# Three layer-norm boundaries of a decoder trunk: two weight residuals ahead of the last norm chain, a reordered first tile, a norm piece cut in two

## The chip, the core and the metric

The kernel runs on one core of a Trainium2 chip. The metric is device time in microseconds (us) of one execution; lower is better. The engines named below are PE (TensorE, matrix products; PEld is its load of the stationary operand), DVE (VectorE), ACT (ScalarE), POOL (GpSimd) and SP (SyncE, which issues nearly all DMAs). Each works through its own instruction list in order and waits on the others by semaphores.

## The reference: what is computed

A two-layer decoder trunk on 256 tokens of width 2048, in float32. Each layer has a token mixer (layer 0 a forgetting attention, "fox"; layer 1 a sliding-window attention, "swa") and a gated feed-forward stage with a short convolution. Every one of the four sub-layers has this form, and the change lies at the joint of two of them:

```python
h = x * (1.0 + sc1) + sh1
y = fox_attention(h, ...)          # or swa_attention, or conv_ffn
x = layer_norm(DEEPNORM_ALPHA * x + (1.0 + g1) * y, ln_mix_g[i], ln_mix_b[i])
h = x * (1.0 + sc2) + sh2
y = conv_ffn(h, ...)
```

The vectors sc, sh and g come from a conditioning vector by a product with a large matrix (`ada_w`), which the kernel forms in the background.

## The kernel before, in words

**Numbers as two parts.** Every float32 operand of a weight product is split into a rounded part and a residual. For a weight pair (two blocks of 128 rows by 512 columns, tile `w`) ACT makes the rounded part `wh` (L276) and DVE the residual `wl = w - wh` (L287). For the activations, `hHL` holds the rounded half hH and the residual half hL, 16 blocks of 128 columns, each by 256 tokens. A product needs three terms: hH by `wh`, hL by `wh`, hH by `wl`. In the feed-forward stages (`w_stationary`, tile `wd`) the weights stand still and hH and hL pass as one operand of 512 columns: 8 products with `wh` of 512 columns and 8 with `wl` of 256 for each pair. In the swa input projection (`x_stationary` with `x_mm`, tile `xs`) the activations stand still: 8 products with `wh` and 4 with `wl`, all of 512 columns.

**The stream.** `stream` issues a pair's load on SP, its rounding on ACT, and puts a closure `go` with its products into the list `work`. `settle(2)` runs the oldest closure while more than two pairs are ahead. Just before a closure runs, `rest` emits the residuals that the next closures need. Tiles `wh` and `wl` have four buffers each (pool `hl`), the loaded `w` ten (pool `wp`).

**The joint.** Between two sub-layers stands a closure put there by `halt` and kept in `stops`: `between`, which calls `modulate`. There are three: fox to feed-forward 0, feed-forward 0 to swa, swa to feed-forward 1. `rest` returns when it meets a stop, so residuals of the next sub-layer's pairs come behind it; those of its first two pairs are in `behind`, which pins them to program order.

**The last norm chain.** The last 512 columns of the old sub-layer's output (`residual` with `end`, L621 to L632) go through DVE token half by token half: times gate, plus x, statistics, aggregate, then POOL raises to the power -1/2. The last pairs of the product before it are kept so that token half 0 ends early (`x_mm_end`). `normalise(d)` (L638) subtracts the mean and scales 512 columns: token half 0 on ACT (L644), token half 1 on DVE (L646). Half 0 of all four pieces runs at once, since ACT comes to them early.

**The modulation.** `modulate` (L500) keeps PE busy with products of ones (`warm`), transposes x blocks 0 to 3 (L508), and `mod_pair(..., fast=True)` makes hHL of them: ACT the rounded half (L478), DVE the whole (L479) and the residual half (L482). The other twelve blocks come two at a time out of the list `feeds`, one with each pair of the new sub-layer: transposes (L469), ACT and DVE (L484, L485), ACT's rounding (L85) and DVE's residual (L86). In front of blocks 4, 8 and 12 stands `norm(k // 4)`, the next 512 columns. `pin` keeps an instruction in program order against other pinned ones; the rest is placed by a scheduler when the kernel is built.

Of the kernel before, what the change touches and what calls it, by code (L numbers as in the profile page):

```python
# [17 lines left out]
P = 128  # L18
# [23 lines left out]
def hybrid_trunk(ctx: ExitStack, tc: tile.TileContext, a: dict, out: bass.AP):  # L42
# [181 lines left out]
    def rest(*items):  # L224

        n = 0
        for f in items:
            if f in stops:
                return
            if f in residuals:  # L230
                residuals[f]()
                n += 1
                if f in behind:
                    return
            elif f in weights:
                n += 1
            if n > 2 - (items[0] not in weights):
                return
# [28 lines left out]

    def stream(wsrc, row0, col, ks, use, spare=0):

        for kc in ks[::2]:  # L270
# [15 lines left out]
            def residual_(w=w, h=h, l=l, go=go):  # L286
                pin(nc.vector.tensor_tensor(l, w, f32(h), op=ALU.subtract), go in behind)  # L287
                del residuals[go]

            if any(f in stops for f in work) and sum(f in behind for f in work) < 2:  # L290
                behind.add(go)
# [5 lines left out]

    def x_mm(ps, kc, h, l, stat, last, first=0, ts=range(NT)):

        for t in ts:  # L300
            for i in range(2):
                xh, xl = stat(kc + i, t)
                mm(ps[t], xh, h[:, i, :], start=kc + i == first)
                mm(ps[t], xl, h[:, i, :])
        feed()
        for t in ts:
            for i in range(2):
                mm(ps[t], stat(kc + i, t)[0], l[:, i, :], stop=kc + i == last)
# [33 lines left out]
    def w_stationary(wsrc, col):  # L342
# [3 lines left out]
        def use(kc, h, l):  # L346
            cells = [(i, f) for i in range(2) for f in range(4)]
            for i, f in cells:
                mm(ps[f], h[:, i, f * P:(f + 1) * P], hHL[:, kc + i].rearrange("p a s -> p (a s)"),
                   start=kc + i == 0)  # L350
            feed()
            for i, f in cells:
                mm(ps[f][:, :S], l[:, i, f * P:(f + 1) * P], hH[:, kc + i, :], stop=kc + i == KC - 1)
# [146 lines left out]
    def modulate(G, B, norm):  # L500

        norm(0)
        warm(10)
        ps = {k: [bank() for _ in range(2)] for k in (0, 2)}
        for t in range(NT):
            for k in ps:
                for j in range(2):
                    pin(nc.tensor.transpose(ps[k][j][:, t * P:(t + 1) * P], x[:, t, (k + j) * P:(k + j + 1) * P], ident))  # L508
            warm(6 - 2 * t)
        for k in ps:  # L510
            mod_pair(G, B, k, [b[:, :S] for b in ps[k]], True)

        def feed_(k):
            if k % 4 == 0:
# [123 lines left out]
    def normalise(d):  # L638

        for t in range(NT):  # L640
            mu, rs, nm = moments[t]
            xs = x[:, t, d * 512:(d + 1) * 512]
            if t == 0:
# [535 lines left out]
```

## Time and profile before

| what | value |
|---|---|
| median of 3 runs | 2253.64 us (2253.16 to 2253.78) |
| the profiled execution | 2253.57 us |
| its span, first to last instruction | 2251.8 us |
| mean granted TensorE clock | 0.996 |
| first joint, fox to feed-forward 0: chain from / first `wd` product | 462.55 / 471.35 us |
| second joint, feed-forward 0 to swa: chain from / first `xs` product | 1216.10 / 1224.18 us |
| third joint, swa to feed-forward 1: chain from / first `wd` product | 1495.64 / 1504.50 us |

The profile is of one execution, and the time around its span is 1.77 us. In a timeline row stand the start and the length in us, the engine, the line, the operation with output and inputs, how many are merged into the row, and in brackets how long the engine had been idle and who released it. A merged row runs from the first start to the last end, and neighbouring instructions of an engine overlap a little. In a row of a stretch stand its bounds and length, the busy time and count of each engine, the granted clock, the DMA share and the rate. In the chain of waits each piece starts where the one before it ends, so its lengths add up.

### The profile page before, as it was taken

The numbers are of one execution on the slowest core, as the hardware profiler recorded it, in microseconds if no ns is written. First come the engines' busy times: TensorE is split into PE (matmuls) and PEld (weight loads), VectorE is DVE, ScalarE is ACT, GpSimd is POOL, SyncE is SP. The second block draws the span as 40 slices with busy tenths as digits, with TensorE's granted clock in tenths as the row PEclk, the third lists the DMA queues.
The fourth block names the chain that finished last, engine by engine and source line by source line (L and its number), as shares of the span: only waits on it lengthen the run. The fifth ranks groups of instructions, "written<-read, shape, count | busy, mean of one in ns | idle before, by whom it ended". The sixth has DMA issues, their size and how long they took to land.

```text
span 2251.8 us, 33349 instructions
## 1 busy us (share of the span) xinstructions
PE 2201.7 (98%) x12196; PEld 1891.1 (84%) x12196; DVE 1853.0 (82%) x2686; ACT 1193.7 (53%) x1873; POOL 20.0 (1%) x51
## 2 busy tenths in 40 slices
PE   6999999999999999999999999999999999999997
PEld 6988998788888888888887788888888888888886
DVE  7989998889988968978978989889988655666766
ACT  4546644355655433655534578646655533555542
POOL 0000000000000000000000000000000000000000
PEclk9999999999999999999999999999999999999999
DMA  9999999868878889878887867678887556666653
GB/s 351 388 369 312 341 380 352 313 222 311 309 242 275 318 295 329 286 225 285 279 306 266 283 208 256 222 250 292 287 273 244 180 194 195 188 189 192 192 191 117
DMA packets 287429, 602.68 MB, mean 268 GB/s; under 512 B 21846, under 2 KB 55576, under 8 KB 286752
## 3 DMA queue, kind: packets, MB, share of 16 engines
q1 hardware_dynamic: 286208, 595.86, 78.0%
q0 software_dynamic: 1056, 4.69, 0.6%
q8 instruction: 95, 1.56, 0.3%
q14 instruction: 70, 0.57, 0.1%
HBM read 598.37 MB, written 2.10 MB: 267 GB/s over the span
## 4 chain that ended last, share of the span: by engine, by line
PE 82%; DVE 8%; DMA 6%; ACT 2%; issue 2%; SPq 0%; POOL 0%; DVEq 0%; ACTq 0%
PE wd L76 43%; PE xs L76 31%; DMA wo<-in_ada_w_dram 4%; PE ws L76 3%; DVE wl L287 3%; DVE acc L406 2%; PE sm L76 1%; DMA w<-in_fox_w_in_dram 1%; PE o L76 1%; PE S L76 1%; ACT wh L276 1%; DVE pr L693 1%; DMA wa<-in_ada_w_dram 0%; PE warm L76 0%; PE T L717 0%
## 5 line engine op out<-in xcount | busy, mean ns | idle before, releaser
L276 ACT CAST wh<-w 128x1024 fp32r<-128x1024 f32 x728 | 764.6, 1051 | 794.5 <-PE wd L76 300.0
L287 DVE TENSOR_TENSOR wl<-w,wh 128x1024 fp32r<-128x1024 f32 x728 | 887.2, 1221 | 292.7 <-ACT wh L276 277.0
L76 PE MATMUL wd<-hHL,wh 128*128 128x512 f32 x2816 | 717.9, 397 | 1.1 <-DVE hHL L482 1.1
L76 PEld LDWEIGHTS wd<-hHL,wh 128*128 128x128 f32 x2816 | 503.5, 188 | 100.1 <-issue 2.9
L76 PEld LDWEIGHTS wd<-hHL,wl 128*128 128x128 f32 x2816 | 373.3, 188 | 32.8 <-DVE wl L287 1.6
L76 PE MATMUL wd<-hHL,wl 128*128 128x256 f32 x2816 | 379.6, 277 | 1.1 <-DVE wl L287 1.1
L406 DVE SCALAR_TENSOR_TENSOR acc<-wa,cact,acc 128x1024 f32<-128x1024 f32 x300 | 380.3, 1277 | 0.0
L76 PE MATMUL xs<-wh,gT 128*128 128x512 f32 x1408 | 350.0, 390 | 0.0
L76 PEld LDWEIGHTS xs<-wh,gT 128*128 128x128 f32 x1408 | 263.4, 188 | 54.1
L76 PE MATMUL xs<-wl,gT 128*128 128x512 f32 x704 | 189.6, 389 | 0.0
L76 PE MATMUL xs<-wh,hHL 128*128 128x512 f32 x704 | 186.1, 401 | 2.9 <-DVE hHL L86 2.7
L76 PEld LDWEIGHTS xs<-wl,gT 128*128 128x128 f32 x704 | 132.1, 188 | 27.6
L76 PEld LDWEIGHTS xs<-wh,hHL 128*128 128x128 f32 x704 | 129.1, 190 | 29.5 <-DVE hHL L86 3.8
L76 PE MATMUL ws<-hHL,wh 128*128 128x256 f32 x1024 | 133.4, 282 | 9.0 <-ACT wh L276 6.6
L1066 ACT ACTIVATE u<-s,ccol 128x256 f32<-128x256 f32 x176 | 104.7, 600 | 66.4 <-DVE s L1061 48.8
L76 PEld LDWEIGHTS ws<-hHL,wh 128*128 128x128 f32 x1024 | 125.1, 190 | 12.7 <-ACT wh L276 8.5
L76 PE MATMUL xs<-wl,hHL 128*128 128x512 f32 x352 | 98.2, 399 | 1.7 <-DVE wl L287 1.7
L76 PE MATMUL xs<-wh,oT 128*128 128x512 f32 x384 | 98.8, 395 | 0.1
L551 DVE SCALAR_TENSOR_TENSOR oacc<-wo,cact,oacc 128x512 f32<-128x512 f32 x111 | 79.7, 746 | 15.3 <-DMA wo<-in_ada_w_dram 14.8
L1067 DVE SCALAR_TENSOR_TENSOR u<-s,ccol,u 128x255 f32<-128x255 f32 x176 | 84.0, 479 | 5.6 <-ACT u L1066 5.4
L1069 DVE SCALAR_TENSOR_TENSOR u<-s,ccol,u 128x254 f32<-128x254 f32 x176 | 83.8, 477 | 1.1
L76 PEld LDWEIGHTS xs<-wh,oT 128*128 128x128 f32 x384 | 69.9, 188 | 13.9 <-ACT pT L719 0.6
(223 smaller groups left out, 1639.5 us busy)
## 6 DMA issues: line engine op xcount, KB each, us to landing
w<-in_ffn_w_up_dram SPq DMA_DIRECT2D x352, 512.0 KB, 4.6
wa<-in_ada_w_dram SPq DMA_DIRECT2D x320, 512.0 KB, 5.1
w<-in_ffn_w_down_dram SPq DMA_DIRECT2D x176, 512.0 KB, 4.3
w<-in_fox_w_in_dram SPq DMA_DIRECT2D x96, 512.0 KB, 6.6
wo<-in_ada_w_dram SPq DMA_DIRECT2D x128, 256.0 KB, 6.7
w<-in_swa_w_in_dram SPq DMA_DIRECT2D x40, 512.0 KB, 5.4
w<-in_fox_w_o_dram SPq DMA_DIRECT2D x32, 512.0 KB, 5.9
w<-in_swa_w_o_dram SPq DMA_DIRECT2D x32, 512.0 KB, 5.3
```

What stands on the lines that cost most here:

```text
L76: return nc.tensor.matmul(o, lhsT, rhs, start=start, stop=stop, **kw)
L276: pin(nc.scalar.copy(h, w), False)
L287: pin(nc.vector.tensor_tensor(l, w, f32(h), op=ALU.subtract), go in behind)
L406: pin(nc.vector.scalar_tensor_tensor(ac, wo, cact[:, k:k + 1], ac, op0=ALU.mult, op1=ALU.add), True)
L551: nc.vector.scalar_tensor_tensor(ac, wk, cact[:, kc:kc + 1], ac, op0=ALU.mult, op1=ALU.add)
L693: nc.vector.tensor_tensor_reduce(pr[:, b:e].rearrange("p (a k) -> p a k", k=P), S_ps[:, b:e].rearrange("p (a k) -> p a k", k=P), mk, -1.0, ...
L1066: nc.scalar.activation(u, s, AF.Identity, bias=cw(CW, f), scale=cw(2, f))
L1067: nc.vector.scalar_tensor_tensor(u[:, 1:], s[:, :S - 1], cw(1, f), u[:, 1:], op0=ALU.mult, op1=ALU.add)
L1069: nc.vector.scalar_tensor_tensor(u[:, 2:], s[:, :S - 2], cw(0, f), u[:, 2:], op0=ALU.mult, op1=ALU.add)
```

## The change

It has four parts, all at the three joints.

1. `rest` no longer returns at a stop. When the last closure ahead of the stop is about to run, it also emits the residuals of the first two pairs behind the stop. `behind` now takes three pairs instead of two, and `tied` pins the next two residuals that are made after `modulate`.
2. The first pair of the new sub-layer (`fresh`) is computed in another order: first all products with hH (with `wh` and with `wl`), then those with hL. In the feed-forward stages hH and hL then pass apart, in 24 products of 256 columns in place of 8 of 512 and 8 of 256.
3. `norm(0)` is cut in two on DVE: 256 columns, then 256 columns, with the transposes of blocks 0 and 1 between them in the text. `norm(1)` comes right behind the two fast pairs, no longer out of `feeds`.
4. The second `warm` has 2 products instead of 4.

```diff
     def rest(*items):
-        n = 0
+        n = past = 0
         for f in items:
             if f in stops:
-                return
+                past = 1
+                continue
+            if past:
+                if f in weights and n <= (items[0] in weights) and past < 3:
+                    past += 1
+                    if f in residuals:
+                        residuals[f]()
+                continue
...
             def residual_(w=w, h=h, l=l, go=go):
-                pin(nc.vector.tensor_tensor(l, w, f32(h), op=ALU.subtract), go in behind)
+                pin(nc.vector.tensor_tensor(l, w, f32(h), op=ALU.subtract), go in behind or tied[0] > 0)
+                tied[0] -= 1
                 del residuals[go]
-            if any(f in stops for f in work) and sum(f in behind for f in work) < 2:
+            if any(f in stops for f in work) and sum(f in behind for f in work) < 3:
                 behind.add(go)
...
     def x_mm(ps, kc, h, l, stat, last, first=0, ts=range(NT)):
+        if fresh[0]:
+            fresh[0] = False
+            for w in (h, l):
+                for i in range(2):
+                    for t in ts:
+                        mm(ps[t], stat(kc + i, t)[0], w[:, i, :], start=w is h and kc + i == first)
+            feed()
+            for i in range(2):
+                for t in ts:
+                    mm(ps[t], stat(kc + i, t)[1], h[:, i, :], stop=kc + i == last)
+            return
...
         def use(kc, h, l):
             cells = [(i, f) for i in range(2) for f in range(4)]
+            if fresh[0]:
+                fresh[0] = False
+                for i in range(2):
+                    for w in (h, l):
+                        for f in range(4):
+                            mm(ps[f][:, :S], w[:, i, f * P:(f + 1) * P], hH[:, kc + i, :], start=w is h and i == 0, skip_group_check=True)
+                feed()
+                for i, f in cells:
+                    mm(ps[f][:, S:], h[:, i, f * P:(f + 1) * P], hL[:, kc + i, :], skip_group_check=True)
+                return
...
     def modulate(G, B, norm):
-        norm(0)
+        fresh[0] = True
+        norm(0, 0)
         warm(10)
         ps = {k: [bank() for _ in range(2)] for k in (0, 2)}
         for t in range(NT):
             for k in ps:
+                if t == 1 and k:
+                    norm(0, 1)
...
-            warm(6 - 2 * t)
+            warm(6 - 4 * t)
         for k in ps:
             mod_pair(G, B, k, [b[:, :S] for b in ps[k]], True)
+        norm(1)
+        tied[0] = 2
         def feed_(k):
-            if k % 4 == 0:
+            if k % 4 == 0 and k > 4:
                 norm(k // 4)
...
-    def normalise(d):
+    def normalise(d, half=None):
         for t in range(NT):
             mu, rs, nm = moments[t]
             xs = x[:, t, d * 512:(d + 1) * 512]
+            if half is not None and t:
+                xs = xs[:, half * 256:(half + 1) * 256]
+            if t == 0 and half:
+                continue
```

**DVE at the second joint, ahead of the last chain.** The rows are DVE's list in program order, `wl` the residuals, `acc` the background product with `ada_w`, `t<-xs,gate` the first instruction of the chain. Before:

```order
L406 SCALAR_TENSOR_TENSOR acc<-wa,cact,acc 128x1024
L287 TENSOR_TENSOR wl<-w,wh 128x1024 x2
L406 SCALAR_TENSOR_TENSOR acc<-wa,cact,acc 128x1024 x3
L621 TENSOR_TENSOR t<-xs,gate 128x512
L622 TENSOR_TENSOR x<-x,t 128x512
```

And in the changed kernel:

```order
L296 TENSOR_TENSOR wl<-w,wh 128x1024 x2
L440 SCALAR_TENSOR_TENSOR acc<-wa,cact,acc 128x1024 x2
L296 TENSOR_TENSOR wl<-w,wh 128x1024 x2
L440 SCALAR_TENSOR_TENSOR acc<-wa,cact,acc 128x1024
L660 TENSOR_TENSOR t<-xs,gate 128x512
L661 TENSOR_TENSOR x<-x,t 128x512
```

Two residuals now stand between the `acc` products, ahead of the chain. At the first and third joints the two stand directly or almost directly ahead of it, with no `acc` near.

**DVE at the first joint, from the end of the chain on.** `x<-x,mv,rs` is `normalise` of token half 1, `t<-sm` the whole and `hHL` the residual half of modulated blocks; rows of 128x256 belong to the fast pairs, blocks 0 to 3. Before:

```order
L646 TENSOR_SCALAR x<-x,mv,rs 128x512
L479 TENSOR_SCALAR t<-sm,G,B 128x256 x2
L482 TENSOR_TENSOR hHL<-t,hHL 128x256 x2
L479 TENSOR_SCALAR t<-sm,G,B 128x256 x2
L482 TENSOR_TENSOR hHL<-t,hHL 128x256 x2
L287 TENSOR_TENSOR wl<-w,wh 128x1024 x2
L646 TENSOR_SCALAR x<-x,mv,rs 128x512
L287 TENSOR_TENSOR wl<-w,wh 128x1024
L485 TENSOR_SCALAR t<-sm,G,B 128x256
L287 TENSOR_TENSOR wl<-w,wh 128x1024
L485 TENSOR_SCALAR t<-sm,G,B 128x256
L86 TENSOR_TENSOR hHL<-t,hHL 128x2x256
```

And in the changed kernel:

```order
L689 TENSOR_SCALAR x<-x,mv,rs 128x256 x2
L513 TENSOR_SCALAR t<-sm,G,B 128x256 x2
L516 TENSOR_TENSOR hHL<-t,hHL 128x256 x2
L513 TENSOR_SCALAR t<-sm,G,B 128x256 x2
L516 TENSOR_TENSOR hHL<-t,hHL 128x256 x2
L689 TENSOR_SCALAR x<-x,mv,rs 128x512
L296 TENSOR_TENSOR wl<-w,wh 128x1024
L519 TENSOR_SCALAR t<-sm,G,B 128x256
L86 TENSOR_TENSOR hHL<-t,hHL 128x2x256
L296 TENSOR_TENSOR wl<-w,wh 128x1024
L519 TENSOR_SCALAR t<-sm,G,B 128x256
L296 TENSOR_TENSOR wl<-w,wh 128x1024
```

The two residuals behind the fast pairs are gone from here, the first piece is cut in two, and `hHL` of blocks 4 and 5 now follows its `t` with no residual between them.

**PE at the first joint, from the second `warm` on.** `sm<-ident,x` are transposes; the four ahead of the `warm` row are token half 1 of blocks 0 to 3. Before:

```order
L76 MATMUL warm<-ones 128x512 x4
L76 MATMUL wd<-hHL,wh 128x512 x8
L469 MATMUL sm<-ident,x 128x128 x4
L76 MATMUL wd<-hHL,wl 128x256 x8
L76 MATMUL wd<-hHL,wh 128x512 x3
```

And in the changed kernel:

```order
L76 MATMUL warm<-ones 128x512 x2
L76 MATMUL wd<-hHL,wh 128x256 x4
L76 MATMUL wd<-hHL,wl 128x256 x4
L76 MATMUL wd<-hHL,wh 128x256 x4
L76 MATMUL wd<-hHL,wl 128x256 x4
L503 MATMUL sm<-ident,x 128x128 x2
L76 MATMUL wd<-hHL,wh 128x256 x8
L76 MATMUL wd<-hHL,wh 128x512 x2
```

The first pair's sixteen products with hH now come first, the two transposes of token half 0 behind them, and the eight products with hL last. SP's and POOL's lists have the same rows in the same order as before.

More of the change, by code (lines that the diff above doesn't have):

```diff
@@ L266, in feed @@
             feeds.pop(0)()
+    tied = [0]
     def stream(wsrc, row0, col, ks, use, spare=0):
@@ L296, in stream @@
             settle(2)
+    fresh = [False]
     def x_mm(ps, kc, h, l, stat, last, first=0, ts=range(NT)):
+        if fresh[0]:
[9 more added lines that the diff above has]
+            return
         for t in ts:
@@ L347, in use @@
             cells = [(i, f) for i in range(2) for f in range(4)]
+            if fresh[0]:
[8 more added lines that the diff above has]
+                return
             for i, f in cells:
                 mm(ps[f], h[:, i, f * P:(f + 1) * P], hHL[:, kc + i].rearrange("p a s -> p (a s)"),
-                   start=kc + i == 0)
+                   start=kc + i == 0, skip_group_check=True)
             feed()
             for i, f in cells:
-                mm(ps[f][:, :S], l[:, i, f * P:(f + 1) * P], hH[:, kc + i, :], stop=kc + i == KC - 1)
+                mm(ps[f][:, :S], l[:, i, f * P:(f + 1) * P], hH[:, kc + i, :], stop=kc + i == KC - 1,
+                   skip_group_check=True)
         stream(wsrc, 0, col, list(range(KC)), use)
```

## The prediction

> **What bounds the kernel now.** I read the page's busy table first, then the busy time by stretch, then the timeline at the joints.
>
> ```profile
> PE 2201.7 (98%) x12196; PEld 1891.1 (84%) x12196; DVE 1853.0 (82%) x2686; ACT 1193.7 (53%) x1873; POOL 20.0 (1%) x51
> ```
>
> That is the whole span. By stretch:
>
> ```profile
> 471.35:491.97 20.62, 19.67 (x114) 16.39 (x115) 20.36 (x30) 11.75 (x17) 0.00 (x0) 1.00 0.70 235
> 491.97:651.00 159.03, 159.03 (x921) 138.67 (x921) 151.22 (x213) 94.56 (x145) 0.00 (x0) 1.00 0.89 303
> 1224.20:1250.00 25.80, 24.01 (x112) 18.48 (x111) 24.18 (x35) 14.73 (x21) 0.00 (x0) 1.00 0.59 186
> 1250.00:1300.00 50.00, 48.47 (x230) 39.07 (x229) 49.17 (x89) 26.72 (x49) 1.36 (x4) 1.00 0.87 295
> 1504.50:1525.10 20.60, 19.64 (x114) 16.37 (x115) 20.13 (x29) 11.77 (x18) 0.00 (x0) 1.00 0.73 242
> 1525.10:1700.00 174.90, 174.90 (x1012) 152.42 (x1011) 159.67 (x231) 103.98 (x161) 0.00 (x0) 1.00 0.84 276
> ```
>
> The columns behind the length are PE, PEld, DVE, ACT, POOL, clock, DMA share and GB/s. Over the whole span PE is the bound, and in the feed-forward stretches (second and last row) it never rests: what a joint saves there comes out of the end in full. In the 20 to 26 us behind each joint DVE is the bound instead: 20.36 of 20.62, 24.18 of 25.80, 20.13 of 20.60 us. Behind the second joint DVE stays so (49.17 of 50.00). The DMA share there is 0.59 to 0.87, below 1, so loads are not what lacks.
>
> **Part 1: two residuals ahead of the chain.** DVE waits for PE ahead of each last chain:
>
> ```profile
> 458.89 1.06 ACT L276 CAST wh<-w 128x1024 fp32r<-128x1024 f32 x1 [1.67 <-DMA wa<-in_ada_w_dram]
> 462.55 0.69 DVE L621 TENSOR_TENSOR t<-xs,gate 128x512 f32<-128x512 f32 x1 [6.78 <-PE xs L76]
> 1209.26 3.67 DVE L406 SCALAR_TENSOR_TENSOR acc<-wa,cact,acc 128x1024 f32<-128x1024 f32 x3
> 1212.47 1.05 ACT L276 CAST wh<-w 128x1024 fp32r<-128x1024 f32 x1 [1.66 <-PE xs L76]
> 1216.10 0.69 DVE L621 TENSOR_TENSOR t<-xs,gate 128x512 f32<-128x512 f32 x1 [3.16 <-PE xs L76]
> 1491.97 1.05 ACT L276 CAST wh<-w 128x1024 fp32r<-128x1024 f32 x1 [2.62 <-DMA w<-in_ffn_w_up_dram]
> 1495.64 0.69 DVE L621 TENSOR_TENSOR t<-xs,gate 128x512 f32<-128x512 f32 x1 [4.94 <-PE xs L76]
> 1236.52 0.46 DVE x L646
> 1239.03 1.13 DVE wl L287
> 1240.16 0.62 DVE hHL L86
> ```
>
> A residual takes 1.13 us of DVE's list (chain of waits, second joint), two 2.26. The idle time is 6.78, 3.16 and 4.94 us, so there is room. A residual needs its `wh` first; the three ACT rows are the second new pair's rounding, done at 459.95, 1213.52 and 1493.02. At the second joint, the tight one, DVE would run two `acc` to 1211.7, a residual to 1212.9, the second from 1213.6 to 1214.8 and the third `acc` to 1216.0, against a chain that starts at 1216.10. I take no delay; its bounds are 0 and one residual, 1.13. If that cover were gone, the chain and all behind it would slide by just that. The saving on DVE behind the joint is 2.26 us each.
>
> **Part 2: the first pair's order.** A pair costs PE the same either way:
>
> ```profile
> 245.37 2.73 PE ws L76 x24
> 651.90 5.55 PE wd L76 x32
> 468.63 0.55 DVE L646 TENSOR_SCALAR x<-x,mv,rs 128x512 f32<-128x512 f32 x1 [0.70 <-POOL rs L632]
> 469.60 1.48 ACT L478 ACTIVATE hHL<-sm,B,G 128x256 fp32r<-128x256 f32 x3 [0.48 <-PE sm L508]
> 469.64 1.17 PE L76 MATMUL warm<-ones 128*128 128x512 f32 x4
> 471.35 2.10 PE L76 MATMUL wd<-hHL,wh 128*128 128x512 f32 x8 [0.53 <-DVE hHL L482]
> 474.43 1.21 PE L76 MATMUL wd<-hHL,wl 128*128 128x256 f32 x8 [0.55 <-DVE wl L287]
> 479.85 0.33 PE L469 MATMUL sm<-ident,x 128*128 128x128 f32 x1 [0.32 <-ACT t L484]
> 474.45 1.05 ACT L276 CAST wh<-w 128x1024 fp32r<-128x1024 f32 x1 [1.86 <-DVE wl L287]
> ```
>
> 24 products of 256 columns take 2.73 us (attention's `ws`), a pair of `wd` 5.55/2 = 2.78. What moves is the start: before, the first product waits for hL until 471.35. Now it needs only hH of block 0, which is ACT's first third of the 469.60 row: some 0.5 us, plus 0.1 to reach PE, so 470.2, less part 3's lead (below) of 0.15: 470.05. That is 1.3 us. The wait for `wl` at 474.43 (0.55) and that at 479.85 (0.32, a place in the list that is now another) go too. PE can thus gain 1.3 + 0.55 + 0.32 = 2.15 us per feed-forward joint, unless DVE stops it later. The price: `wh` of pair 0 is held to that pair's end, 470.05 + 2.73 and two transposes, some 473.0, and ACT's next rounding waits for it; before, it waited for the late residual until 474.45 (last row), so nothing is lost.
>
> **Parts 3 and 4: the cut piece, the shorter `warm`.** A 256-column piece of `normalise` is not in the trace. It lies between the same operation's 512 columns and a one-column one of the same kind:
>
> ```profile
> L646 DVE TENSOR_SCALAR x<-x,mv,rs x12: 540/542/548, 468.6 to 1520.4; 128x512 f32<-128x512 f32 x12
> L629 DVE TENSOR_SCALAR rs<-mv x8: 153/154/155, 465.0 to 2243.0; 128x1 f32<-128x1 f32 x8
> 469.71 1.03 DVE L479 TENSOR_SCALAR t<-sm,G,B 128x256 f32<-128x256 f32 x2 [0.53 <-PE sm L508]
> ```
>
> So 0.154 to 0.542 us; I take 0.39, nearer to the large one, since an operation of 256 columns out of PSUM takes about as much (1.03 for two). The first transposes start 0.15 us sooner (bounds 0 and 0.39). The second piece ends at about 469.3, and DVE idles until 469.71 anyway (0.53), so the second instruction's fixed cost is hidden there; without that gap it would cost 0.24. [...]
>
> Two `warm` products fewer free 2 x 1.17/4 = 0.6 us of PE, but that `warm` ended ahead of a wait (0.53 before 471.35). It only makes room for the earlier start.
>
> **What DVE leaves of it.** DVE bounds the stretch, so the list order decides. I follow each list to the residual half of blocks 8 and 9, the fifth pair's input, with pitches 1.13 (residual), 0.46 (`x`, and `t` alike), 0.62 (`hHL`).
>
> ```profile
> 1230.24 0.69 DVE L86 TENSOR_TENSOR hHL<-t,hHL 128x512 fp32r<-128x512 f32 x1 [0.74 <-ACT hHL L85]
> 479.37 0.69 DVE L86 TENSOR_TENSOR hHL<-t,hHL 128x512 fp32r<-128x512 f32 x1 [0.22 <-ACT hHL L85]
> 1226.77 1.15 DVE wl L287
> 1236.52 0.46 DVE x L646
> ```
>
> The new order has one bad place: `hHL` directly behind its `t`. ACT's rounding lies between, and DVE stands still: 0.74 us in the one place where before has this order (second joint), 0.22 with a residual between (first). So:
> - First joint: two residuals fewer (-2.26), one `t` moved ahead (+0.46), the stall (0.74-0.22 = +0.52), the lead (-0.15): **-1.45 us**. That is less than PE's 2.15, so DVE decides.
> - Third joint: there a third residual moves behind that point (-3.39), +0.52, -0.15: -3.0. PE's own **-2.15** decides.
> - Second joint: before, DVE needs 1236.52-1226.77 = 9.75 us from the end of the fast pairs to the third piece of `x`. After, that way holds three residuals, one `x`, two `t`, two `hHL`: 3.39+0.46+0.92+1.24 = 6.0 us, and stalls for transposes and ACT that I put at 1.45 (a walk with the lists; bounds 0 and 3.2, where nothing would be gained but half a microsecond). So 2.3, with the lead 2.45; I take **-2.3** for its thin cover in part 1. Behind it the lists are the same, and every load that DVE releases goes out earlier by as much.
>
> SP issues no DMA more or less. Its loads behind the chain wait for the first residuals' `w`, which is free some 13 us sooner; the queue has room there.
>
> **Sum.** 1.45 + 2.3 + 2.15 = 5.9 us off the profiled 2253.57, which lies 0.07 under the median of 2253.64: **2247.7 us**, 0.26% faster. A measurement of this kernel can tell about 0.2%, 4.5 us, from no change, so faster begins at 2249.1.
>
> **The rivals.**
> - *The swa stage keeps the second joint's share.* Its input projection and heads wait on DVE, ACT and DMA in turn; a lead of DVE can end in one of their waits. For it: PE has gaps from 1250 on (48.47 of 50.00). Against: the lists there are unchanged, and DVE is at 98%. It gives 5.9-2.3 = 3.6: 2250.0.
> - *The order binds less than I say.* The stalls are covered and each joint gains DVE's 2.26 to 3.0: some 8.7 in all, 2244.9. Against it stands the 0.74 row.
> - *PE cools.* The rows show cold products:
>
> ```profile
> 16.97 2.48 PE L76 MATMUL warm<-ones 128*128 128x512 f32 x5
> 25.12 2.10 PE L76 MATMUL ws<-hHL,wh 128*128 128x256 f32 x16 [2.00 <-ACT wh L276]
> 465.10 2.44 PE L76 MATMUL warm<-ones 128*128 128x512 f32 x10
> ```
>
>   Five take as long as ten do later, at the start of the program; after a wait of 2.00 us they are at full speed. With half of a `warm` gone a joint could cool, at 2.48-2.44/2 = 1.26 us each time, 3.8 in all: 2251.5. It decides at a PE wait longer than 2.00 us; my walk has none over 1.3. [...]
> - *Slower: the residuals hold up the chain.* DVE is in order. If the two ahead of the chain are of pairs whose `wh` buffers are held by the kept last pairs, their rounding comes only when PE lets go:
>
> ```profile
> 456.17 1.05 ACT L276 CAST wh<-w 128x1024 fp32r<-128x1024 f32 x1 [1.67 <-PE xs L76]
> 464.83 1.05 ACT L276 CAST wh<-w 128x1024 fp32r<-128x1024 f32 x1 [0.32 <-PE xs L76]
> ```
>
>   The second row is such a rounding. Then the residual ends at 465.88+1.2 = 467.1 and the chain starts there, not at 462.55: 4.55 us at each joint, 13.7-5.9 = +7.8: 2261.4. It decides where a rounding ends later than about 1.2 us ahead of the chain. Against it: the roundings of the first two new pairs lie at 456.17 and 458.89, and the list has just these two more ahead of the chain.
> - That the change doesn't do what it says is excluded for part 1, which the lists show at all three joints. For part 3 it is likely to be invisible.
>
> **How the numbers follow.** Chances: forecast 0.58, swa keeps its share 0.22, binds less 0.10, cooling 0.05, held up 0.05. Faster by over 0.2%: 0.58+0.10 = 0.68; within 0.2%: 0.22+0.05 = 0.27; slower: 0.05. The forecast's own range is 2246.0 to 2249.0 (stalls at the second joint, cover of the tight `acc`). The range reaches from the third case (2244.9) to 1.5 us above the second: 2244.8 to 2251.5; outside lie the last case and edges of the others.
>
> **What would show it.** Right: each chain starts as far behind its last `xs` product as now; the first `wd` product comes 7.5 us after the chain's start instead of 8.8 (471.35-462.55), with no wait for `wl`; DVE idles some 0.7 us ahead of the first `hHL` of 128x512; the second joint's third `x` piece comes 2.3 us sooner after the chain's start, and the output projection of swa too. Wrong: DVE rows `t<-xs,gate` released by a residual, a granted clock under 1.00 behind a joint, or a swa stage longer by what its joint saved.

## The result, and the profile after

The changed kernel takes **2248.78 us**, median of 14 runs (2246.59 to 2251.35), beside 2253.69 us for the kernel before in the same comparison (14 runs, 2251.40 to 2254.79). The ratio is **0.9978, 95% interval 0.9971 to 0.9986**: 4.9 us, or 0.22%, faster. The profiled execution took 2247.84 us, its span is 2246.1 us.

First the page's busy line of the changed kernel (busy time of each engine, its share of the span, its instructions):

```profile
PE 2199.2 (98%) x12206; PEld 1890.7 (84%) x12206; DVE 1854.0 (83%) x2689; ACT 1194.2 (53%) x1873; POOL 19.9 (1%) x51
```

The engines do the same work as before, to 2.5 us of PE and 1.0 us of DVE. What went is time in which PE waited or turned `warm` products. The place is read best from the starts of the three last chains. These are the changed kernel's timeline rows of DVE (start, busy time, line, operation, idle time ahead of it and what ended that); the first row of each chain is `t<-xs,gate`. Ahead of the first chain stand the two residuals that now lie there, ahead of the second the later of the two and the `acc` behind it:

```profile
457.47 1.23 DVE L296 TENSOR_TENSOR wl<-w,wh 128x1024 fp32r<-128x1024 f32 x1 [1.49 <-ACT wh L285]
460.19 1.23 DVE L296 TENSOR_TENSOR wl<-w,wh 128x1024 fp32r<-128x1024 f32 x1 [1.50 <-ACT wh L285]
462.76 0.69 DVE L660 TENSOR_TENSOR t<-xs,gate 128x512 f32<-128x512 f32 x1 [1.34 <-PE xs L76]
...
1212.21 1.23 DVE L296 TENSOR_TENSOR wl<-w,wh 128x1024 fp32r<-128x1024 f32 x1 [0.69 <-ACT wh L285]
1213.35 1.28 DVE L440 SCALAR_TENSOR_TENSOR acc<-wa,cact,acc 128x1024 f32<-128x1024 f32 x1
1214.75 0.69 DVE L660 TENSOR_TENSOR t<-xs,gate 128x512 f32<-128x512 f32 x1
...
1492.05 0.69 DVE L660 TENSOR_TENSOR t<-xs,gate 128x512 f32<-128x512 f32 x1 [1.35 <-PE xs L76]
```

The residuals fit into the idle time (6.78 us before the first chain, now 1.34), and the first and third chains are still released by PE. At the second joint the third `acc` ends at 1213.35 + 1.28 = 1214.63 and the chain follows at 1214.75 with no idle time shown: the cover there is used up to the last tenth, but the chain is not held: the last `xs` product ahead of the joint starts 2.29 us after the chain's start, as before (2.32 at the other two joints, also as before).

Before, the same three rows stood at 462.55, 1216.10 and 1495.64 us, in a span of 2251.8. So up to the first chain the changed kernel was 0.21 us later, at the second 1.35 earlier, at the third 3.59 earlier, at the end 5.7 earlier. The stretch behind joint 1 (with all of ffn0) gave -1.56 us, that behind joint 2 (with all of swa) -2.24, that behind joint 3 (with all of ffn1) -2.11. All runs below are read in this way, because single executions differ ahead of the first joint: a second profile of the very same changed kernel had its first chain at 464.57 instead of 462.76, 1.8 us later, and ended 1.7 us later, while its three stretches came out at -1.55, -2.30 and -2.17, within 0.06 us of the first profile. By this one pair of profiles a stretch is known to about 0.1 us, a whole run only to 1 or 2. The shift is made at the joint: from 55 us behind the first chain on, every `wd<-hHL,wl` product of ffn0, matched one by one with before's, starts 1.56 us sooner after the chain.

Behind the first joint, the changed kernel's PE and DVE rows (two timelines in order of time, columns as above):

```profile
468.84 0.74 DVE L689 TENSOR_SCALAR x<-x,mv,rs 128x256 f32<-128x256 f32 x2 [0.70 <-POOL rs L671]
469.84 1.03 DVE L513 TENSOR_SCALAR t<-sm,G,B 128x256 f32<-128x256 f32 x2 [0.26 <-PE sm L545]
470.38 0.71 PE L76 MATMUL wd<-hHL,wh 128*128 128x256 f32 x4
471.39 0.63 PE L76 MATMUL wd<-hHL,wh 128*128 128x256 f32 x4
471.87 0.64 PE L76 MATMUL wd<-hHL,wl 128*128 128x256 f32 x4
476.16 0.69 DVE L86 TENSOR_TENSOR hHL<-t,hHL 128x512 fp32r<-128x512 f32 x1 [0.74 <-ACT hHL L85]
484.43 0.68 DVE L86 TENSOR_TENSOR hHL<-t,hHL 128x512 fp32r<-128x512 f32 x1
485.17 2.13 PE L76 MATMUL wd<-hHL,wh 128*128 128x512 f32 x8
```

The first `wd` product starts 470.38 - 462.76 = 7.62 us after the chain, before 8.80. The stall of `hHL` directly behind its `t` is there, with the very 0.74 us that the forecast took. The fifth pair's products start at 485.17, right behind their last input, the residual half done at 484.43 + 0.68 = 485.11: PE waits for DVE on the way, which is why its start alone does not decide.

### The profile page after: what moved, and what is told of

It reads as the page before. It is cut to its first block, busy times and chain, and to the rows that moved or that the text cites. A ratio compares the mean times of both kernels' runs of the same rounds, so it can differ in the third digit from the quotient of the medians.

```text
span 2246.1 us, 33371 instructions
## 1 busy us (share of the span) xinstructions
PE 2199.2 (98%) x12206; PEld 1890.7 (84%) x12206; DVE 1854.0 (83%) x2689; ACT 1194.2 (53%) x1873; POOL 19.9 (1%) x51
## 3 DMA queue, kind: packets, MB, share of 16 engines
q8 instruction: 95, 1.56, 0.3%
## 4 chain that ended last, share of the span: by engine, by line
PE 81%; DVE 8%; DMA 7%; ACT 2%; issue 2%; SPq 0%; POOL 0%; DVEq 0%; ACTq 0%
PE wd L76 43%; PE xs L76 31%; DMA wo<-in_ada_w_dram 3%; DVE acc L440 3%; DVE wl L296 2%; PE ws L76 2%; DMA w<-in_fox_w_in_dram 2%; PE sm L76 1%; PE o L76 1%; PE S L76 1%; ACT wh L285 1%; PE warm L76 1%; DVE pr L736 0%; PE T L760 0%; ACT pr L748 0%
## 5 line engine op out<-in xcount | busy, mean ns | idle before, releaser
L76 PE MATMUL wd<-hHL,wh 128*128 128x512 f32 (+1 forms) x2832 | 718.2, 395 | 0.2
```

The lines of the kernel that those rows point to most:

```text
L76: return nc.tensor.matmul(o, lhsT, rhs, start=start, stop=stop, **kw)
```

## Experiments

The change and ten other kernels were run, two of them twice, in five comparisons on several chips, each with its own runs of the kernel before. So times are compared within a comparison, and across them only by their ratios. The shift of each stretch against before is worked out from the `t<-xs,gate` rows and the span of its profile, as above (for the run whose profile is of no use, see there). "Time" is the median of its runs, "ratio" that to the kernel before of the same comparison.

| kernel | time, us | ratio, 95% interval | joint 1 + ffn0 | joint 2 + swa | joint 3 + ffn1 |
|---|---|---|---|---|---|
| the change | 2248.78 | 0.9978, 0.9971 to 0.9986 | -1.56 | -2.24 | -2.11 |
| the change again | 2249.40 | 0.9979, 0.9970 to 0.9988 | -1.55 | -2.30 | -2.17 |
| residuals only | 2249.96 | 0.9983, 0.9974 to 0.9992 | -1.16 | -2.31 | -1.00 |
| without residuals | 2256.85 | 1.0012, 1.0003 to 1.0021 | +1.36 | +0.55 | +1.04 |
| old product order, first time | 2247.67 | 0.9971, 0.9961 to 0.9982 | no profile | | |
| old product order, second time | 2247.04 | 0.9970, 0.9959 to 0.9982 | -1.39 | -3.13 | -2.02 |
| piece not cut | 2247.24 | 0.9973, 0.9961 to 0.9985 | -1.57 | -3.01 | -1.45 |
| four warm products | 2247.18 | 0.9968, 0.9955 to 0.9980 | -1.65 | -3.01 | -1.93 |
| no warm products | 2255.18 | 1.0005, 0.9996 to 1.0015 | +0.60 | -0.84 | +1.63 |
| late half | 2246.93 | 0.9968, 0.9956 to 0.9981 | -2.82 | -2.30 | -1.90 |
| late half, four warm | 2246.31 | 0.9968, 0.9956 to 0.9980 | -2.65 | -3.03 | -1.99 |
| late half, four warm, not cut | 2246.28 | 0.9968, 0.9956 to 0.9979 | -2.52 | -2.80 | -1.80 |
| late half, four warm, not cut, old order | 2248.02 | 0.9975, 0.9966 to 0.9985 | -1.70 | -2.89 | -1.46 |

### The residuals alone

The product order, the cut piece, the shorter `warm` and the moved second piece of `x` are undone:

```diff
 def modulate(G, B, norm):
-        fresh[0] = True
-        norm(0, 0)
+        norm(0)
...
-                if t == 1 and k:
-                    norm(0, 1)
...
-            warm(6 - 4 * t)
+            warm(6 - 2 * t)
...
-        norm(1)
-        tied[0] = 2
...
-            if k % 4 == 0 and k > 4:
+            if k % 4 == 0:
```

> Residuals of the first two new pairs ahead of the last chain alone; first pair's order, whole norm piece, late second piece and four warm products as before. My theory (each joint gains the smaller of what DVE's list saves and what PE can start earlier): the first product still waits for hL, so PE's own gain at the first and third joints is only the vanished waits, 0.55 + 0.32 = 0.9 us each; at the second, where DVE decides, about 2.2. In all 4.0 us faster than before, 2249.7. Rival, the first pair's order makes the gain: at most 1.5 us faster. Rival, DVE's lead counts in full everywhere: 2.3 at each joint, 6.8 us.

Measured: 4.15 us faster than before (2249.96 beside 2254.11), stretches -1.16, -2.31 and -1.00. The whole gain of the second joint, three quarters of the first's and half of the third's belong to the two residuals. DVE's rows of this kernel at the first joint, and one of PE, show why it is not 2.26 there:

```profile
475.23 1.22 DVE L296 TENSOR_TENSOR wl<-w,wh 128x1024 fp32r<-128x1024 f32 x1
476.37 0.54 DVE L684 TENSOR_SCALAR x<-x,mv,rs 128x512 f32<-128x512 f32 x1
476.82 1.22 DVE L296 TENSOR_TENSOR wl<-w,wh 128x1024 fp32r<-128x1024 f32 x1
477.96 0.54 DVE L519 TENSOR_SCALAR t<-sm,G,B 128x256 f32<-128x256 f32 x1
478.41 1.22 DVE L296 TENSOR_TENSOR wl<-w,wh 128x1024 fp32r<-128x1024 f32 x1
480.39 0.69 DVE L86 TENSOR_TENSOR hHL<-t,hHL 128x512 fp32r<-128x512 f32 x1 [0.31 <-ACT hHL L85]
481.13 2.13 PE L76 MATMUL wd<-hHL,wh 128*128 128x512 f32 x8
```

Two residuals still stand among the first blocks' work, and a third follows the first `t`: where before had four of them ahead of the first `hHL` of 512 columns, this list has three. The scheduler orders the list behind the joint anew, and one of the two that went out comes back from further down. The last row is the third pair's products; they start right behind that `hHL` (480.39 + 0.69 = 481.08). So DVE's list decides here, and the gain is one residual (1.13); the theory's 0.9 was close, but not for its reason, the vanished waits of PE.

### Everything but the residuals

```diff
             if f in stops:
-                past = 1
-                continue
+                return
...
-            if any(f in stops for f in work) and sum(f in behind for f in work) < 3:
+            if any(f in stops for f in work) and sum(f in behind for f in work) < 2:
```

> The change without its residuals ahead of the chain; all else kept. My theory: PE starts 1.3 us earlier with four products, then stands in order at the first residual, which DVE finishes behind the fast pairs and the second norm piece, at about 474.8 on the first joint's clock against 474.4 before; twenty products still follow, so the feed-forward joints lose 0 to 1.5 us each and the second is even: 0 to 3 us slower than before, 2253.7 to 2256.7. Rival, the first pair's order makes the gain by itself: 4 us faster.

Measured: slower than before, ratio 1.0012 (1.0003 to 1.0021), with every stretch later. The timeline of PE at its first joint, and behind it one row of the busy time by stretch (PE, PEld, DVE, ACT, POOL, granted clock, DMA share, GB/s):

```profile
473.48 0.48 PE L502 MATMUL sm<-ident,x 128*128 128x128 f32 x2 [1.04 <-DVE t L512]
474.73 0.66 PE L502 MATMUL sm<-ident,x 128*128 128x128 f32 x4 [0.78 <-DVE x L688]
475.72 0.48 PE L502 MATMUL sm<-ident,x 128*128 128x128 f32 x1 [0.33 <-ACT t L517]
475.87 1.22 PE L76 MATMUL wd<-hHL,wl 128*128 128x256 f32 x4
476.88 1.05 PE L76 MATMUL wd<-hHL,wh 128*128 128x256 f32 x4
477.74 1.05 PE L76 MATMUL wd<-hHL,wl 128*128 128x256 f32 x4
```

```profile
475.90:482.00 6.10, 6.10 (x34) 5.74 (x34) 5.94 (x7) 2.23 (x4) 0.00 (x0) 0.77 0.79 260
```

The new order puts products with the residual `wl` at once behind the first four. With the residuals late, these come at 475.87 only; PE goes idle three times on the way, 2.15 us together, and the granted clock falls to 0.77. Four products of 256 columns and the next four then start 0.86 us apart (476.88 and 477.74), where the changed kernel's start 0.48 apart (471.39 and 471.87, quoted above). So the rest of the change, the new order in it, is no gain by itself; it needs the residuals ahead of the chain. How much of the loss is the late residuals, how much the clock, and what the two `warm` products fewer add to it, this run doesn't separate.

### The old product order, all else as changed

```diff
-        fresh[0] = True
         norm(0, 0)
```

> The change without the first pair's new order; all else kept. My theory: first product 0.15 us earlier than before instead of 1.0, so PE's own gain is 1.0 at the first and third joints and DVE's 2.2 at the second: 4.2 us faster than before, 2249.5; the order is then worth about 1.7 us on top of the residuals. Rival, the order makes the gain: even with before. Rival, DVE decides all three joints: as fast as the whole change, 2248.8.

Measured: 2247.67 us, ratio 0.9971 (0.9961 to 0.9982), not slower than the change. One of its eight executions took 5674.91 us, the other seven 2246.75 to 2250.41, and the profile is of the long one (last section). The same kernel a second time:

> The first pair's products in the order of before, all else as in the change. Theory (PE's own gain of 1.3 us from the earlier start decides at the third joint, DVE's list at the first and second): joint 1 -1.5, joint 2 -2.1, joint 3 -0.9 us, 4.5 in all, 2249.2, 1.3 slower than the change. Rival (DVE's list decides all three joints): every joint within 0.3 us of the change's, and the time within 0.5 of the change's in the same comparison. Second rival (the order is the whole gain of joints 1 and 3 beyond the residuals' -1.15 and -1.04): joints 1 and 3 at -1.1 each, 4.4 in all.

Measured: 2247.04 us, ratio 0.9970 (0.9959 to 0.9982), beside 2249.40 of the change itself in the same comparison; stretches -1.39, -3.13 and -2.02. The timeline of PE and DVE at its first joint, where the chain starts at 461.19:

```profile
461.19 0.69 DVE L659 TENSOR_TENSOR t<-xs,gate 128x512 f32<-128x512 f32 x1 [1.34 <-PE xs L76]
469.91 2.11 PE L76 MATMUL wd<-hHL,wh 128*128 128x512 f32 x8 [0.94 <-DVE hHL L516]
474.58 0.69 DVE L86 TENSOR_TENSOR hHL<-t,hHL 128x512 fp32r<-128x512 f32 x1 [0.74 <-ACT hHL L85]
```

The first product starts 8.72 us after the chain, 1.1 later than with the new order, and yet the stretch loses only 0.17 us at joint 1 and 0.09 at joint 3: the stall of 0.74 stands at the same distance from the chain (13.39 us, in the change 13.40), and PE, which waits less on its way (0.42 us ahead of the fifth pair, in the change 0.63), has nearly caught up behind it: its fifth pair's first product comes 0.77 us later after the chain than the change's, its seventh's 0.18. The first theory (joint 3 falls to -0.9) and the second rival are both out. The first rival fits at joints 1 and 3: when PE starts decides neither. Its own terms aren't met in full, since the second joint and the time came out better than the change's, and from 17 to 20 us behind these two chains on DVE's lists are not the same in the two kernels. Of the 2.4 us between the two medians, the stretches hold 0.5; the rest lies ahead of the first joint.

The second joint came out 0.8 us better than in the change, which no theory had. DVE's rows behind it, of the change:

```profile
1228.33 0.54 DVE L519 TENSOR_SCALAR t<-sm,G,B 128x256 f32<-128x256 f32 x1 [0.96 <-PE sm L503]
1229.49 0.69 DVE L86 TENSOR_TENSOR hHL<-t,hHL 128x512 fp32r<-128x512 f32 x1 [0.62 <-ACT hHL L85]
```

and of this kernel:

```profile
1226.83 0.54 DVE L519 TENSOR_SCALAR t<-sm,G,B 128x256 f32<-128x256 f32 x1 [0.85 <-PE sm L503]
1227.29 0.68 DVE L86 TENSOR_TENSOR hHL<-t,hHL 128x512 fp32r<-128x512 f32 x1
```

One wait of 0.85 us in place of 0.96 + 0.62 = 1.58. The second wait is ACT's order. Here is ACT in the change, and below it in the kernel with the old order (both timelines):

```profile
1227.89 1.05 ACT L285 CAST wh<-w 128x1024 fp32r<-128x1024 f32 x1 [0.56 <-PE xs L76]
1228.85 0.61 ACT L85 CAST hHL<-t 128x512 fp32r<-128x512 f32 x1
```

```profile
1225.12 0.57 ACT L518 ACTIVATE t<-sm,B,G 128x256 f32<-128x256 f32 x1 [0.42 <-PE sm L503]
1226.07 0.62 ACT L85 CAST hHL<-t 128x512 fp32r<-128x512 f32 x1 [0.38 <-DVE t L519]
```

In the change a rounding of weights, which itself waits for PE (0.56), stands on ACT between the `t` and the rounding `hHL` that DVE needs next. That the kernels with the uncut piece, with four warm products and with the late half and four warm products have a second stretch of -3.01 to -3.03 too, and one wait less in their rows there (0.86 to 0.89), fits this; the exchange on ACT was never made by itself, it came as a by-product of the scheduler's rule, so its price of 0.7 to 0.8 us is read from rows, not isolated.

### The piece not cut, and more or no warm products

```diff
-        norm(0, 0)
+        norm(0)
...
-                if t == 1 and k:
-                    norm(0, 1)
```

> The change with the first 512 columns normalised in one piece; all else kept. My theory: the first transposes of token half 1 come 0.1 to 0.15 us later and everything behind them with it, three times: 0.3 to 0.45 us slower than the change, less than the times can tell, but visible as the first product's distance from the chain's start. Rival by the fixed cost of each instruction: the two pieces cost as much as they save, no difference.

Measured: 2247.24 us, ratio 0.9973 (0.9961 to 0.9985), against the change's 0.9978: no difference that a measurement tells. Joint 1 is unchanged (-1.57). Joints 2 and 3 moved in opposite directions, since the scheduler's lists behind them changed with the edit, so these two say nothing on the cut. In the change the first `t` behind the cut piece starts 469.84 - 468.84 = 1.00 us after it, before 1.08 after the whole one (469.71 - 468.63). The first product comes 7.67 us after the chain instead of 7.62.

```diff
-            warm(6 - 4 * t)
+            warm(6 - 2 * t)
```

> The change with four products of ones in the second warm-up; all else kept. My theory: they run to about 0.35 us behind the moment at which the first block's rounded half is there, so the first product comes 0.35 us later; that counts only at the third joint, where PE decides: 0.3 us slower than the change in all, not to be told by the times. Rival, the clock: no difference at all or faster, if two products were too few to hold the clock.

Measured: 2247.18 us, ratio 0.9968 (0.9955 to 0.9980). The first product comes 8.07 us after the chain instead of 7.62, and yet the two products more cost nothing that can be seen: joint 1 at -1.65, joint 3 at -1.93, each within 0.2 us of the change.

The `warm` products' result is not used. This kernel has none at the joints:

```diff
-        warm(10)
...
-            warm(6 - 4 * t)
```

> The change with no products of ones at the joints at all. It leaves out only those. PE then stands still about 2.3 us at the end of the old products, then 1.2 us, then 0.6 us. My theory: after a wait of 2.0 us the products were at full speed in the kernel before, so the clock holds and the time is that of the change, within 0.3 us. Rival, the clock falls: the first products behind each joint take twice as long, 1.3 us or more at each, 3.8 us or more slower than the change, and the granted clock behind the joints is under 1.00.

Measured: 2255.18 us, ratio 1.0005 (0.9996 to 1.0015): all that the change had won is gone, as the rival said. The timeline of the chain's first row and of PE behind the first joint, and one row of the busy time by stretch:

```profile
461.86 0.69 DVE L658 TENSOR_TENSOR t<-xs,gate 128x512 f32<-128x512 f32 x1 [1.34 <-PE xs L76]
466.37 0.66 PE L544 MATMUL sm<-ident,x 128*128 128x128 f32 x4 [1.80 <-ACT x L685]
468.40 0.77 PE L544 MATMUL sm<-ident,x 128*128 128x128 f32 x4 [1.37 <-DVE x L687]
469.38 0.74 PE L76 MATMUL wd<-hHL,wh 128*128 128x256 f32 x4 [0.22 <-ACT hHL L512]
470.77 1.05 PE L76 MATMUL wd<-hHL,wh 128*128 128x256 f32 x4
471.62 1.05 PE L76 MATMUL wd<-hHL,wl 128*128 128x256 f32 x4
```

```profile
471.50:475.00 3.50, 3.50 (x22) 3.32 (x21) 2.47 (x5) 0.98 (x2) 0.00 (x0) 0.72 0.00 0
```

The first product comes at 469.38 - 461.86 = 7.52 us after the chain, as early as with `warm`, but the granted clock falls to 0.72 and the products start 0.85 us apart by fours (470.77 and 471.62) instead of 0.48. The other two joints have the same two waits (1.81 and 1.37, 1.85 and 1.39 us). The longest of these six waits is 1.85 us, below the 2.00 us from which the forecast let the cooling decide.

### The residual half of hHL one place later

This takes the stall of `hHL` behind its `t` away. Behind the first and third joints, in blocks 4 to 13, the subtraction that makes `hHL`'s residual half is issued behind the next weight residual, at the latest ahead of the next pair's products; nothing else is changed:

```diff
+    late, lag = [], [False]
+    def flush_late():
+        while late:
+            late.pop(0)()
...
                 del residuals[go]
+                flush_late()
...
                 fed[0] = False
+                flush_late()
                 use(kc, h, l)
...
-        split(hH[:, k:k + 2, :], hL[:, k:k + 2, :], tmp.rearrange("p (j s) -> p j s", j=2))
+        src = tmp.rearrange("p (j s) -> p j s", j=2)
+        nc.scalar.copy(hH[:, k:k + 2, :], src)
+        low = lambda: pin(nc.vector.tensor_tensor(hL[:, k:k + 2, :], src, f32(hH[:, k:k + 2, :]), op=ALU.subtract))
+        late.append(low) if lag[0] and 4 <= k <= 12 else low()
...
+        lag[0] = v == 3
         modulate(*merged(l, v, g, b, ll), normalise)
```

> The change, and at the two feed-forward joints DVE's residual half of blocks 4 to 13 is written behind the next weight residual instead of right behind its own whole part, so that ACT's rounding between them is covered. My theory: the 0.74 us stall of DVE goes, the fifth pair's input is about 1.2 us sooner at the first joint, which then gains PE's own 2.15 instead of 1.5; the third stays at PE's 2.15 and the second as it is: 0.6 us faster than the whole change. Rival, the first joint is bound by something else than DVE's list (PE's late start, transposes): no difference, first joint 1.5.

Measured: 2246.93 us, ratio 0.9968 (0.9956 to 0.9981). Joint 1 gives -2.82, 1.26 us more than the change, and more than the 2.15 that the forecast held to be PE's own limit; joint 3 gives 0.2 less than the change. The third `hHL` of 512 columns, the fifth pair's input, now starts 484.01 - 463.67 = 20.34 us after the chain (with four warm products as well 483.26 - 462.92 = 20.34), in the change 484.43 - 462.76 = 21.67. These 1.33 us are the stall (0.74), one `t` (0.46) that the list now has behind this point, and 0.1 of small gaps; so the stall is worth about its length, and the rest is the list's new order. At joint 3, where the same stall of 0.74 stood (`hHL` at 1505.46), the edit brought nothing: the first `hHL` comes 1506.02 - 1491.64 = 14.38 us after the chain, in the change 13.41, since an `acc` and a residual now stand ahead of it, and the third pair's products wait for it (timeline of the late half):

```profile
1506.76 2.14 PE L76 MATMUL wd<-hHL,wh 128*128 128x512 f32 x8 [0.45 <-DVE hHL L530]
```

With four warm products as well, and the change itself beside it:

> The late residual half at the first and third joint together with six warm products more in all (four behind the second transposes as before, not two). Theory (the stall behind t is DVE's at joints 1 and 3, warm products lie ahead of a wait): as the late half alone, joints -2.8, -2.1 and -1.9, 1 us faster than the change, 2247 to 2248. Rival (PE's own start limits once DVE's stall is gone, so two warm products cost their 0.6 us at joints 1 and 3): equal to the change within 0.3 us.

> The change itself, beside the others in one comparison. Expected of all theories: 4.9 us faster than before (2248.8), joints -1.6, -2.1 and -2.2 us by the trace, as in its first profile. If the joints come out otherwise by over 0.3 us, single profiles do not tell kernels apart by so little, and the rows of the other experiments are to be read with that width.

Measured: 2246.31 us (six runs, 2245.09 to 2247.89), ratio 0.9968 (0.9956 to 0.9980), beside 2249.40 of the change (eleven runs, 2246.26 to 2250.55). The stretches sum to -7.67 against -6.02. The theory held at joints 1 and 3; joint 2 came out 0.7 us better than it said. By the stretches this is the best of the versions, by 1.65 us in the profiles and 3.1 us in the medians; the intervals of the two ratios to before overlap.

From there the cut piece was undone, and then the product order too:

> As the late half with four warm products, and the first token-half-1 piece in one instruction of 512 columns instead of two of 256. Theory (the cut's lead of at most 0.15 us a joint ends in waits that are there anyway): within 0.3 us of the kernel with the cut. Rival (the cut's lead counts once DVE's stall is gone): 0.15 to 0.35 us later at joints 1 and 3, 0.3 to 0.7 us slower in all, which only the trace could tell.

> The late residual half with four warm products, the first token-half-1 piece whole, and the first pair's products in the order of before; of the change there remain the two residuals ahead of the chain and the second x piece's new place. DVE's list at the first and third joint is that of the late half with the new order. Theory (behind the joint DVE's list alone decides, when PE starts does not): joints -2.6, -2.7 and -1.9 us as with the new order, 7.3 in all, 2246 to 2247.5. Rival (with DVE's stall gone PE's own start limits, and the new order's 1.1 us counts): joints 1 and 3 each 0.7 to 1.1 us worse, -1.7, -2.7 and -1.0, 5.4 in all, about 2248.2.

Measured: without the cut 2246.28 us, and joint 1 -2.52 instead of -2.65, joint 3 -1.80 instead of -1.99: 0.13 and 0.19 us for the cut, at two joints where DVE's lists differ by nothing but the cut. That is little more than two profiles of one kernel differ by; DVE's own rows show 0.09 and 0.14 at the third `hHL`. With the old order besides, 2248.02 us (ratio 0.9975, 0.9966 to 0.9985), joint 1 at -1.70 and joint 3 at -1.46, 0.8 and 0.3 us worse, with no difference at joint 2: the rival was right at joint 1, and at joint 3 got half of what it said. DVE's list at the joints is the same in these two kernels, so it is PE that lags. The last kernel's rows of both engines:

```profile
462.80 0.69 DVE L667 TENSOR_TENSOR t<-xs,gate 128x512 f32<-128x512 f32 x1 [1.34 <-PE xs L76]
471.60 2.11 PE L76 MATMUL wd<-hHL,wh 128*128 128x512 f32 x8 [0.53 <-DVE hHL L523]
477.44 0.55 DVE L526 TENSOR_SCALAR t<-sm,G,B 128x256 f32<-128x256 f32 x1 [0.17 <-PE sm L510]
484.64 2.03 PE L76 MATMUL wd<-hHL,wh 128*128 128x512 f32 x8
```

The chain starts at 462.80 in it, so the fifth pair's products come 484.64 - 462.80 = 21.84 us after the chain. In the kernel with the new order (and the piece not cut either) they come, by the same two timelines, at

```profile
465.67 0.69 DVE L668 TENSOR_TENSOR t<-xs,gate 128x512 f32<-128x512 f32 x1 [1.34 <-PE xs L76]
...
486.89 2.11 PE L76 MATMUL wd<-hHL,wh 128*128 128x512 f32 x8
```

with the chain at 465.67: 21.22 us. And now DVE waits for PE (0.17). The same new order that was worth 0.17 us at joint 1 beside the stall is worth 0.8 without it (at joint 3 0.09 and 0.3).

## Why the prediction came out as it did

The forecast of 2247.7 us lies 1.1 us under the measured median, and the profiled execution, on which the sum was made, is at 2247.84. The three terms were 1.45, 2.3 and 2.15 us, the stretches gave 1.56, 2.24 and 2.11. The first two came about as the forecast said; the third is in part luck. Point by point:

- **The residuals ahead of the chain: right.** They went into idle time at all three joints and delayed no chain; the rival by which they hold it up has no row (the first and third chains are released by PE, as before, and all three start as far ahead of the last `xs` product as before). Alone they gave 4.5 us by the stretches, so they carry most of the change.
- **Joint 1, DVE decides: right, and for the reason given.** The third `hHL` of 512 columns came 485.56 - 462.55 = 23.01 us after the chain before, and 21.67 now: 1.34 sooner, which is two residuals less one `t` and the stall's growth from 0.22 to 0.74, with half of the lead that was forecast for the cut. The fifth pair's products follow it.
- **Joint 3, "PE's own -2.15 decides": right in size, wrong in its reason.** The row that this step looked at came as forecast: the third `hHL` of 512 columns starts 1512.18 - 1492.05 = 20.13 us after the chain, before 1518.69 - 1495.64 = 23.05, so 2.92 sooner for the forecast 3.0, and the fifth pair's products start 0.8 us after it is done. But what PE does ahead of that isn't its own. With the old order, which puts PE's start 1.1 us back, joint 3 still gave -2.02, so PE's start did not set it. The walk followed DVE only to the fifth pair's input; PE meets DVE one pair earlier. There it waits for the third piece of `x`, and the fourth pair's products start right behind the second `hHL` (blocks 6 and 7, done at 1509.99 + 0.69 = 1510.68). Two timelines of the change, in order of time:

```profile
1509.99 0.69 DVE L86 TENSOR_TENSOR hHL<-t,hHL 128x512 fp32r<-128x512 f32 x1
1510.06 0.66 PE L503 MATMUL sm<-ident,x 128*128 128x128 f32 x4 [0.33 <-DVE x L689]
1510.74 2.13 PE L76 MATMUL wd<-hHL,wh 128*128 128x512 f32 x8
```

  That DVE's 2.11 us there lie so near to PE's 2.15 is luck.

- **PE's own limit of 2.15 us per joint: too small.** It added the start and two waits at the places they had before. The late half reached 2.82 at joint 1, and even there the fifth pair's products start at 484.75, right behind DVE's half (484.01 + 0.68 = 484.69; with four warm products at 484.06, behind 483.26 + 0.68 = 483.94), so PE's own limit lies beyond that. Start and counted waits make 1.18 + 0.55 + 0.32 = 2.05 of the 2.82; the rest isn't broken down.
- **Joint 2: right.** The stalls taken at 1.45 us measure 0.96 + 0.62 = 1.58. The third piece of `x` comes 1232.97 - 1214.75 = 18.22 us after the chain's start, before 1236.44 - 1216.10 = 20.34: 2.1 sooner, where 2.3 was said. What the forecast did not see is that 0.6 of these stalls come from ACT's order.
- **swa keeps its share: fell.** The stretch from the second chain to the third lost the 2.24 us in full; matched one by one with before's, PE's products of swa keep the offset that the joint leaves them to 0.1 us, from some 60 us behind the chain on.
- **The first product 7.5 us after the chain: 7.62.** The start of 8.80 moved by 1.18, forecast 1.3. But the step from there to the joint's gain failed: beside the stall, that start is worth 0.17 us at joint 1 and 0.09 at joint 3.
- **The cut: mis-sized, harmless.** Two pieces take 0.74 us (forecast 0.78), but the first `t` shows a lead of 0.08, not 0.15. With the stall gone it shows as 0.1 to 0.2.
- **PE cools: it did not, but the deciding point was wrong.** With its `warm` products the changed kernel kept a granted clock of 1.00 behind all three joints. The point was put at one wait longer than 2.00 us, from a row with one such wait at full speed (16 products 0.12 us apart, at a granted clock of 1.00 from 25.12 to 27.22 us); without `warm` products, two waits of 1.80 and 1.37 us, with 0.66 us of work between them, took the clock to 0.72. So in these rows the longest single wait doesn't decide. The profile of before has a fall of its own, which the forecast didn't use: behind one wait of 2.37 us, ahead of the product at 402.58, its granted clock was 0.50 from 403.19 to 406.60. How long PE must idle, and over what stretch, before the clock falls isn't shown by these runs. Nor do the five slow products at the start of the program, which the forecast called cold, show a lowered clock: they took 0.50 us each, at a granted clock of 1.00 from 16.97 to 19.45 us.
- **The median.** By the stretches the change takes off 5.9 to 6.0 us, by the medians 4.9 and 4.2. The rest lies ahead of the first joint, where PE's, DVE's and ACT's lists are those of before up to the two residuals. The change's first chain started at 462.76 and 464.57 us in two executions, before's at 462.55 in one, and in all twelve profiles with some part of the change it lies between 461.19 and 465.67. So single executions scatter there by more than what is missing; whether the changed program's opening is also later in the mean stays open, with one profile of before.
- **One rival's sum.** The 8.7 us of the rival in which the order binds less aren't added up in the prediction; three joints of 2.26 to 3.0 us make 6.8 to 9.0. It didn't come: the stall stood.

## What to carry to other kernels

When two engines bind one stretch in turn, price each edit with and without the others: here an earlier start on PE was worth 0.2 us at the first joint beside a 0.74 us stall on DVE and 0.8 without it, and without the residuals the rest of the change made the kernel slower. Follow the list that decides to every place where the other engine needs it, not to one: at the third joint the two met a pair earlier than the forecast looked. Look in the rows for a consumer directly behind its own producer with another engine's step between them (`t`, ACT's rounding, then `hHL`): one unrelated instruction put there gave 1.3 us at the first joint, though nothing at the third, where it made the first half late. And where an edit lets a scheduler order its lists anew, compare the lists before half a microsecond is put down to the edit.

## What was not expected of the hardware

- Two waits of 1.80 and 1.37 us with 0.66 us of transposes between them brought the granted clock to 0.72, and four products of 256 columns from 0.48 to 0.85 us, although the longest single wait was shorter than one of 2.00 us, in the profile of before, behind which the products ran at full speed (granted clock 1.00).
- One execution of the kernel with the old product order took 5674.91 us instead of 2247. In its profile a `wd` product of 512 columns takes 831 ns in the mean, in the changed kernel 395, at a recorded clock of 1.00 (line, operation, shapes, count, busy time, mean ns):

```profile
L76 PE MATMUL wd<-hHL,wh 128*128 128x512 f32 x2816 | 1769.1, 831 | 0.0
```

No other execution of any kernel here did this, and no row explains it.
